# A two-layer encoder trunk in split fp32: Strassen's seven products for 18 of 22 up-projection pairs of the FFN

## Chip, cores and metric

One core of a Trainium2 chip runs the whole program. The metric is the device time of one execution in microseconds, as the median of several runs. Times of single instructions and waits come from one profiled execution of the kernel.

## The reference, cut to what matters

The trunk has two layers (DEPTH = 2). It is applied to 512 prompt tokens and 256 sample tokens, each with 1024 features. A layer is a mixer with four attention branches and gates, and then a gated FFN with a depthwise convolution of width 3 over the tokens. The change touches the FFN:

```python
def _conv_ffn(h, w_up, conv_w, conv_b, w_down):
    u = jnp.einsum('bsd,df->bsf', h, w_up)              # 1024 -> 2 * 2816
    up = jnp.pad(u, ((0, 0), (p, p), (0, 0)))           # p = 1
    c = conv_b
    for j in range(CONV_W):                             # CONV_W = 3
        c = c + up[:, j:j + S] * conv_w[j]
    gate, val = jnp.split(c, 2, axis=-1)
    return jnp.einsum('bsf,fd->bsd', jax.nn.gelu(gate, approximate=True) * val, w_down)
```

Around it stand an RMSNorm before (its output is h) and an RMSNorm and the residual add after. All of it is in float32.

## The kernel before

**Layout.** Features lie on the 128 partitions, and the 768 tokens of both groups side by side on the free axis. Each float32 operand x of a matrix product is split exactly into h = float32r(x) and l = x - h. ScalarE makes h by a copy (`copy`, L412) and VectorE makes l by a subtraction (`tt`, L426). A product is accumulated as h*h + h*l + l*h, which is three passes per block of 128 contraction rows. `mblock` issues, for each contraction block and pass, one matmul of 512 columns (prompt) and one of 256 (sample), all by `mm` (L396).

**Weights.** They come in units of [128, 1024] (`unit_keys`) through SyncE's one DMA queue (`dma`, L445) into two `raw` buffers (the two `bi` buffers serve as well at times). `pump` issues the load as soon as a buffer is free, and then splits the unit into one of four `w` buffers. An up-projection unit holds one block of 128 output features over all 8 contraction blocks.

**The FFN** (`ffn`, `up_pair`, `up_start`) has 22 hidden blocks f. For each there is a gate block (up unit f) and a value block (up unit f + 22), together a pair: 2 x 8 x 3 x 2 = 96 matmuls. `conv_block` brings an up block from PSUM through the convolution: a ScalarE copy with scale and bias (tap 1) and two VectorE operations (`stt`, L430; taps 0 and 2) for each token group. `glu` makes gelu(gate) * value and splits it into a `g` buffer. The hidden blocks are used in three parts (`THIRDS`: 7, 7 and 8 blocks). After a part's pairs come its eight output blocks of the down projection, which are added up in four `g` buffers:

```python
THIRDS = ((0, 7), (7, 14), (14, 22))
        for t, (a, b) in enumerate(THIRDS):
            ...
            for f in range(a0, min(b + 1, NF)):
                yield from self.up_pair(f, gs)
```

The last part goes through `grouped_tail`: its first two output blocks run over all tokens, the other six token group by token group, with the norm of each group started as it ends. Six weight units of that tail are split into parts of the next layer's `h` (`tail_h`, `Part`).

**What sets the order.** The program is emitted by generators (`Flow`), in the order of an estimate of the engines' times that is written in the kernel. The order within each engine's queue is then fixed: an engine works strictly along its list, and semaphores do the rest. Buffers have fixed numbers: 13 `g`, 12 `p` (of 512 columns), 4 `w`, 2 `raw`, 2 `bi`, one `h`; in PSUM two double banks `d` and four single banks `b`.

Of the kernel before, what the change touches and what calls it, by code (L numbers as in the profile page):

```python
# [17 lines left out]
F32 = mybir.dt.float32  # L18
# [44 lines left out]
def unit_keys():  # L63
    """The weight units of a layer in the order of their use."""
# [18 lines left out]
    for t, (a, b) in enumerate(THIRDS):  # L83
        a += t > 0
        for f in range(a, min(b + 1, NF)):
            u += [("up", f), ("up", f + NF)]
        u += [("down", t, m) for m in range(KB)]
    return u


def unit_data(key, w_in, w_branch, w_out, w_up, w_down):
    """The unit as [128, n]: contraction rows on partitions, then k block, then output column."""
# [28 lines left out]
    a, b = THIRDS[key[1]]  # L121
    return block(w_down[128 * a : 128 * b], 128 * key[2], 128 * key[2] + 128)


def unit_cols(key):
    if key[0] == "down":
        a, b = THIRDS[key[1]]
        return 128 * (b - a)
    return 1024


def host_arrays(inputs, depth):
# [31 lines left out]
    # rpb laid out by (column, row offset, key column), NEG outside the column window  # L164
# [8 lines left out]
    # constants of the shapes  # L173
# [30 lines left out]
# blocks of w_out and of the last third of the FFN that are computed token group by token group  # L204
# [42 lines left out]
class Slots:  # L247
    """The buffers of one tag: counts the live ones and knows when a free one may be written."""
# [51 lines left out]

class Pair:
    """Weights whose two parts lie in two buffers."""
# [13 lines left out]
class Part:  # L316
    """Weights in the columns of h whose tokens come to be known only after the weights' use."""
# [45 lines left out]
def mixed(a, b):  # L363
    """The elements of a and b, each in its order, evenly mixed, a first."""
# [4 lines left out]
class Trunk:  # L369
# [23 lines left out]
    def mm(self, out, lhsT, rhs, start, stop, *deps):  # L393
        n = out.shape[-1]
        ns = n * 0.4218 * (4 if lhsT.dtype == F32 else 1)
        self.nc.tensor.matmul(out=out, lhsT=lhsT, rhs=rhs, start=start, stop=stop)  # L396
# [55 lines left out]
    def w_init(self):  # L452
# [6 lines left out]
        self.tail_keys |= {("down", 2, m) for m in range(KB - TAIL_DOWN, KB)}  # L459
        self.w_total = self.depth * len(self.keys)  # L460

    def pump(self):
        while self.w_fetched < self.w_total and (self.RAW.freed or self.parts and self.BI.freed):
            n = self.w_fetched
            key = self.keys[n % len(self.keys)]
            tail = key in self.tail_keys
# [5 lines left out]
        while self.w_split < min(self.w_fetched, self.w_allowed):  # L472
            n = self.w_split
            raw, c, tail = self.w_raw[n]
            x = slice(0, c)
            src = raw[:, x]
            if raw.t > self.f.now + 300:
                break
            if tail and self.parts:
                w = self.parts.pop(0)  # L480
                src = src.rearrange("p (k x) -> p k x", x=GRP)
            elif self.W.freed:
                w = self.W.take([128, 2, 1024], F32R)
            elif self.spare and len(self.BI.freed) == 2:
                w = Pair([self.BI.take([128, 1024], F32R) for _ in range(2)])
            else:
                break
            del self.w_raw[n]
            t = self.copy(w[:, 0, x], src, raw.t, w.t)
            t = self.tt(w[:, 1, x], src, w[:, 0, x].bitcast(F32), ALU.subtract, t)  # L490
            w.t = t
            raw.drop(t)
            self.w_ready[n] = w
            self.w_split += 1

    def weight(self, key):
        n = self.w_used
        assert self.keys[n % len(self.keys)] == key, (key, self.keys[n % len(self.keys)])
        self.w_used += 1
        while n not in self.w_ready:  # L500
            self.pump()
            if n not in self.w_ready:
                raw = self.w_raw.get(n)
                yield max(self.f.now + 100, raw[0].t - 300 if raw else 0)
        w = self.w_ready.pop(n)
# [21 lines left out]

    def dblock(self):
# [3 lines left out]
    def bank(self):  # L532
        """A bank, of a double one or, if that leaves one for the norms, a single one."""
# [4 lines left out]
    def anyblock(self):  # L538
        """As dblock, but in two single banks if they are free sooner."""
# [1074 lines left out]
```

## Time and profile before

| | us |
|---|---|
| median of 3 runs (lowest to highest) | 2583.24 (2583.02 to 2583.34) |
| profiled execution, first to last instruction | 2580.6 |
| around that span (median less span) | 2.6 |
| TensorE matmuls busy | 2543.3 (99%) |
| VectorE busy | 1458.1 (57%) |
| ScalarE busy | 1133.5 (44%) |

The profile calls TensorE's matmuls PE and its weight loads PEld; DVE is VectorE, ACT is ScalarE and SP is SyncE, whose queue issues all DMAs. A busy share is the union of an engine's instructions over the span. Matmuls overlap each other, so the mean duration of one is longer than the time from one to the next. A name such as w<-raw tells which tile an instruction writes and reads, with buffer numbers left out. L396 is line 396 of the kernel.

The FFN of layer 0 runs from about 742 to 1240 us and that of layer 1 from about 2018 to 2514 us.

### The profile page before, as it was taken

Reading aid. Unit: us, or ns where it says so; the run is one execution under the profiler, and the core shown is the slowest. Engines: PE = TensorE matmul, PEld = TensorE weight load, DVE = VectorE, ACT = ScalarE, POOL = GpSimd, SP = SyncE. Lnnn points to the kernel's source line nnn. Section 1 sums busy time; section 2 is a strip of 40 time slices with the busy share of each in tenths; the row PEclk is TensorE's granted clock in tenths of the full one; section 3 lists DMA queues with packets and bytes.
Section 4 is the critical chain, followed back from the end, with each engine's and each line's share of the span. In section 5 each row is a group of like instructions: output and inputs, shape, how many; then the busy total and the mean of one; then the engine's idle time right before and its main releaser. Section 6 shows DMA issues by size and latency. Waiting matters only on the chain.

```text
span 2580.6 us, 39698 instructions
## 1 busy us (share of the span) xinstructions
PE 2543.3 (99%) x15964; PEld 2281.7 (88%) x15964; DVE 1458.1 (57%) x2766; ACT 1133.5 (44%) x2166; POOL 39.8 (2%) x38
## 2 busy tenths in 40 slices
PE   7999999999999999999999999999999999999998
PEld 7898888888998888888998988888889988888888
DVE  5567667746475335345566665775565752453554
ACT  5465666522463323233545556654225532331342
POOL 0001000000000000000000000000000000000000
PEclk9999999999999999999999999999999999999999
DMA  3333244433331111111333333443423212112122
GB/s 130 108 116 104 90 145 132 134 134 102 111 103 62 61 66 59 65 66 58 123 96 99 107 109 112 134 135 121 159 70 129 91 54 70 65 52 72 58 82 82
DMA packets 113576, 249.43 MB, mean 97 GB/s; under 512 B 13168, under 2 KB 56816, under 8 KB 113392
## 3 DMA queue, kind: packets, MB, share of 16 engines
q1 hardware_dynamic: 113392, 246.90, 29.7%
q8 instruction: 125, 2.05, 0.3%
q14 instruction: 59, 0.48, 0.1%
HBM read 194.15 MB, written 33.82 MB: 88 GB/s over the span
## 4 chain that ended last, share of the span: by engine, by line
PE 95%; DVE 3%; ACT 1%; issue 1%; DMA 0%; SPq 0%; POOLq 0%; DVEq 0%; ACTq 0%
PE d L396 78%; PE b L396 14%; PE b L400 3%; DVE g L426 1%; DVE p L426 1%; ACT p L412 1%; ACT g L412 0%; DVE h L426 0%; DVE w L426 0%; DVE p L967 0%; ACT w L412 0%; DMA par<-par 0%; ACT h L412 0%; DVE p L430 0%; SPq L445 0%
## 5 line engine op out<-in xcount | busy, mean ns | idle before, releaser
L396 PE MATMUL d<-h,w 128*128 128x512 f32 (+1 forms) x7248 | 1328.2, 338 | 0.0
L396 PEld LDWEIGHTS d<-h,w 128*128 128x128 f32 x7248 | 1106.4, 189 | 148.5
L426 DVE TENSOR_TENSOR w<-raw,w 128x1024 fp32r<-128x1024 f32 (+1 forms) x216 | 260.5, 1208 | 282.2 <-ACT w L412 271.2
L396 PE MATMUL d<-g,w 128*128 128x256 f32 (+1 forms) x2196 | 376.4, 329 | 1.6 <-ACT g L412 1.5
L430 DVE SCALAR_TENSOR_TENSOR p<-d,par,p 128x511 f32<-128x511 f32 (+1 forms) x328 | 204.3, 623 | 292.1 <-ACT p L412 286.3
L396 PEld LDWEIGHTS d<-g,w 128*128 128x128 f32 x2196 | 324.0, 189 | 43.3 <-ACT g L412 2.1
L412 ACT ACTIVATE p<-d,par 128x512 f32<-128x512 f32 (+1 forms) x164 | 111.1, 677 | 384.9 <-PE d L396 255.3
L412 ACT ACTIVATE w<-raw 128x1024 fp32r<-128x1024 f32 (+1 forms) x216 | 224.0, 1039 | 116.7 <-PE d L396 105.6
L412 ACT ACTIVATE p<-p,st 128x512 f32<-128x512 f32 (+2 forms) x288 | 178.1, 629 | 121.1 <-DVE st L994 67.9
L412 ACT ACTIVATE g<-d 128x128 fp32r<-128x128 f32 (+3 forms) x136 | 77.8, 574 | 284.7 <-PE d L396 247.9
L396 PE MATMUL d<-h,bi 128*128 128x256 f32 (+1 forms) x912 | 160.0, 334 | 0.0
L396 PEld LDWEIGHTS d<-h,bi 128*128 128x128 f32 x912 | 137.1, 189 | 19.1
L426 DVE TENSOR_TENSOR p<-b,p 128x512 fp32r<-128x512 f32 (+1 forms) x160 | 103.2, 658 | 63.1 <-ACT p L412 62.5
L412 ACT ACTIVATE p<-b 128x512 fp32r<-128x512 f32 (+1 forms) x160 | 90.6, 574 | 96.4 <-PE b L400 95.5
L396 PE MATMUL b<-g,g 128*128 128x512 f32 (+2 forms) x384 | 107.6, 356 | 2.7 <-DVE p L426 1.8
L396 PE MATMUL d<-g,bi 128*128 128x512 f32 (+1 forms) x636 | 107.7, 326 | 0.0
L396 PEld LDWEIGHTS d<-g,bi 128*128 128x128 f32 x636 | 93.0, 189 | 11.1
L396 PE MATMUL d<-w,h 128*128 128x256 f32 x672 | 93.7, 296 | 8.2 <-ACT h L412 3.4
L396 PE MATMUL b<-p,g 128*128 128x256 f32 x608 | 99.1, 287 | 1.1 <-DVE p L426 1.1
L412 ACT ACTIVATE g<-p 128x512 fp32r<-128x512 f32 x112 | 56.5, 540 | 98.1 <-DVE p L426 64.5
L967 DVE CUSTOM_DVE_ANT_0 p<-b,bi 128x512 f32<-128x512 f32 (+1 forms) x144 | 85.9, 597 | 22.5 <-PE b L396 18.1
L396 PEld LDWEIGHTS d<-w,h 128*128 128x128 f32 x672 | 88.3, 202 | 10.7 <-ACT h L412 4.0
(104 smaller groups left out, 2454.1 us busy)
## 6 DMA issues: line engine op xcount, KB each, us to landing
raw<-weights SPq DMA_DIRECT2D x236, 512.0 KB, 3.6
raw<-weights SPq DMA_DIRECT2D x32, 448.0 KB, 3.3
g<-g SPq DMA_DIRECT2D x128, 96.0 KB, 2.2
x<-g SPq DMA_DIRECT2D x36, 256.0 KB, 2.1
p<-x SPq DMA_DIRECT2D x36, 256.0 KB, 4.1
bi<-na_bias SPq DMA_DIRECT2D x64, 128.0 KB, 2.8
p<-x_in SPq DMA_DIRECT2D x24, 256.0 KB, 5.3
g<-g SPq DMA_DIRECT2D x16, 384.0 KB, 3.6
```

Source lines behind the costliest of these rows:

```text
L396: self.nc.tensor.matmul(out=out, lhsT=lhsT, rhs=rhs, start=start, stop=stop)
L400: self.nc.tensor.transpose(out=out, in_=in_, identity=self.ident)
L412: self.nc.scalar.activation(out=out, in_=in_, func=func, **k)
L426: self.nc.vector.tensor_tensor(out=out, in0=a, in1=b, op=op)
L430: self.nc.vector.scalar_tensor_tensor(out=out, in0=a, scalar=s, in1=b, op0=op0, op1=op1)
L967: nc.vector.tensor_tensor_reduce(out=p[:, :nkey], in0=s[:, :nkey], in1=bt, scale=1.0, scalar=init, op0=ALU.add, op1=ALU.max, accum_out=mx[ ...
```

## The change

Pairs 0 to 3 (`PLAIN = 4`) stay as they were. Pairs 4 to 21 are computed by `up_forms` with seven products in place of eight (Strassen's scheme in Winograd's form). The contraction is halved (512 and 512 rows), the tokens are halved (`TH` = 384 columns), and gate block and value block are the two halves of the output. A product is 4 contraction blocks x 3 passes = 12 matmuls of 384 columns (`mprod`), and a pair is 84 matmuls.

- `forms` makes, once per layer, four differences of h's quarters (8 `g` buffers, kept till the last pair).
- `preparer` makes, for each pair, four sums and differences of the weights' quarters on VectorE, and splits seven weight blocks in place of eight.
- `up_forms` brings the products together in an SBUF buffer u: four ScalarE copies out of PSUM and three VectorE adds of PSUM onto u, each of 384 columns. Two PSUM regions, x and z, each accumulate several products in turn, with a copy or an add between them.
- Each gate block goes through convolution and gelu (`gate_block`). For ten hidden blocks (`WHOLE`) the value block is convolved and multiplied at once, and the product goes to DRAM. For the other twelve the gelu and the raw value block go to DRAM, and the value's convolution is done on return (`value_block`, `g_load`).
- All 22 pairs now come before the down projection. It has five parts (`CHUNKS`: 2, 8, 2, 2 and 8 blocks). `g_loader` fetches the hidden blocks from DRAM in that order, each into a `g` buffer when one is free. The eight blocks of the second part (`BANK`) go into the `h` buffer, once the up projection has ended. The last part goes through `grouped_tail` as before.
- `calm` holds back an instruction for VectorE while the estimate has more than 0.5 us queued there.

```diff
-THIRDS = ((0, 7), (7, 14), (14, 22))
+WHOLE = (0, 1, 6, 8, 10, 12, 14, 16, 18, 20)
+CHUNKS = (WHOLE[:2], WHOLE[2:], (2, 3), (4, 5), (7, 9, 11, 13, 15, 17, 19, 21))
+BANK = WHOLE[2:]
+PLAIN = 4
+TH = T // 2
...
+    def preparer(self):
...
+            done(w, (yield from self.calm_split(w, all_, raw.ap, raw.t)))
...
+            t = self.tt(s1.ap, raw2[:, lo], raw2[:, hi], ALU.add, raw2.t, s1.t)
+            t2 = self.tt(s2.ap, s1.ap, raw[:, lo], ALU.subtract, t, s2.t)
+            yield from self.calm_split(w, hi, s2.ap, t2)
+            done(w, (yield from self.calm_split(w, lo, s1.ap, t)))
+            yield from self.calm()
+            t = self.tt(raw2[:, lo], raw[:, lo], raw2[:, lo], ALU.subtract)
+            t2 = self.tt(s1.ap, raw[:, hi], s2.ap, ALU.subtract)
...
+            t = yield from self.calm_split(w, all_, raw2.ap, t)
...
+            t = yield from self.calm_split(w, lo, s1.ap, t2)
...
+    def mprod(self, out, w, i, rhs, start):
+        for k in range(4):
+            c = 512 * i + 128 * k
+            for n, (a, b) in enumerate(self.PASSES):
+                t = self.mm(out, w[:, a, c : c + 128], rhs(k, b), start and k == 0 and n == 0,
+                            k == 3 and n == 2, more=not start)
...
+    def up_forms(self, f):
...
+        x, z, y1 = d[:, 0:TH], d[:, 512 : 512 + TH], y[:, 0:TH]
+        t = yield from self.mprod(x, w, 0, quarter(0, lo), True)
+        t1 = self.copy(u[:, 0, lo], x, t, u.t)
+        t = yield from self.mprod(y1, w, 1, quarter(4, lo), True)
...
+        t1 = self.tt(u[:, 0, lo], u[:, 0, lo], y1, ALU.add, t, t1)
...
+        t = yield from self.mprod(x, w, 1, summed(1), False)
+        t2 = self.copy(u[:, 0, hi], x, t, u.t)
...
+        t = yield from self.mprod(z, w, 0, summed(0), True)
...
+        t3 = self.copy(u[:, 1, hi], z, t, u.t)
...
+        t = yield from self.mprod(x, w, 0, summed(2), False)
+        t3 = self.tt(u[:, 1, hi], u[:, 1, hi], x, ALU.add, t, t3)
...
+        t = yield from self.mprod(z, w2, 0, quarter(4, hi), False)
...
+        t2 = self.tt(u[:, 0, hi], u[:, 0, hi], z, ALU.add, t, t2)
+        self.up_done(f, Summed(u, 0, max(t1, t2)))
...
+        t = yield from self.mprod(x, w, 1, summed(3), False)
...
+        t4 = self.copy(u[:, 1, lo], x, t, u.t)
...
+    def g_load(self, f, q, c0, c1, box):
...
+        v.t = t = self.dma(v[:, 0:n], dv[:, c0:c1], v.t)
+        if f not in WHOLE:
+            a.t = self.dma(a[:, 0:n], da[:, c0:c1], a.t)
...
+            t = yield from self.conv(f + NF, v[:, 0:n], c, n, v.t)
...
+            t = self.tt(c[:, 0:n], c[:, 0:n], a[:, 0:n], ALU.mult, t, a.t)
...
+        t = self.copy(q.ap[:, 0, c0:c1], c[:, 0:n], t, q.t)
...
+        t = self.tt(q.ap[:, 1, c0:c1], c[:, 0:n], q.f32()[:, 0, c0:c1], ALU.subtract, t)
...
     def ffn(self, gain, sandwich, box):
         gs = [[] for _ in range(NF)]
...
+        yield from self.up_start()
+        for f in range(2, PLAIN):
+            yield from self.up_pair(f)
+        self.f.start(self.g_loader(gs), 2)
+        for f in range(PLAIN, NF):
+            yield from self.up_forms(f)
...
+        for n, fs in enumerate(CHUNKS):
```

**TensorE in one pair of layer 0.** In the up projection before, the matmuls alternate between 512 and 256 columns through a block, and 48 of them make a block (d152 is the gate block of pair 11, w107 its weights):

```order
L396 MATMUL d152_11058<-h2_6736,w103_10807 128x512
L396 MATMUL d152_11058<-h2_6736,w103_10807 128x256
L396 MATMUL d153_11129<-h2_6736,w104_10877 128x512 [waits DVE_49,Activation_49]
L396 MATMUL d153_11129<-h2_6736,w104_10877 128x256
L396 MATMUL d153_11129<-h2_6736,w104_10877 128x512
```

Now pair 17 reads as follows (d119 holds x and z, b313 is y1, g91 to g98 are the differences of h, w106 to w108 and g127 the prepared weights):

```order
L441 MATMUL d119_10091<-h2_6736,w106_9979 128x384 x12
L441 MATMUL b313_10092<-h2_6736,w106_9979 128x384 x12
L441 MATMUL d119_10091<-g93_8123,w107_9995 128x384 [waits Activation_49]
L441 MATMUL d119_10091<-g93_8123,w107_9995 128x384 x5
L441 MATMUL d119_10091<-g94_8148,w107_9995 128x384 x6
L441 MATMUL d119_10091<-g91_7860,w107_9995 128x384 [waits Activation_49]
L441 MATMUL d119_10091<-g91_7860,w107_9995 128x384 x5
L441 MATMUL d119_10091<-g92_7885,w107_9995 128x384 x6
L441 MATMUL d119_10091<-g95_8185,w108_10041 128x384 [waits Activation_49]
L441 MATMUL d119_10091<-g95_8185,w108_10041 128x384 x5
L441 MATMUL d119_10091<-g96_8207,w108_10041 128x384 x6
L441 MATMUL d119_10091<-h2_6736,g127_10062 128x384 [waits DVE_49]
```

A product's twelve matmuls now stand together, and where x or z is used again the first matmul waits for ScalarE's copy or VectorE's add of the product before.

**VectorE ahead of the last part of the down projection, layer 0.** Before, these are the rows from the convolution of the last value block (d157, pair 21) to the split of its product into g115, the last hidden block of the last part:

```order
L430 SCALAR_TENSOR_TENSOR p471_11465<-d157_11396,par0_103,p471_11465 128x511 [waits Activation_49]
L430 SCALAR_TENSOR_TENSOR p471_11465<-d157_11396,par0_103,p471_11465 128x511 [waits DVE_49]
L430 SCALAR_TENSOR_TENSOR p472_11469<-d157_11396,par0_103,p472_11469 128x255 [waits Activation_49]
L430 SCALAR_TENSOR_TENSOR p472_11469<-d157_11396,par0_103,p472_11469 128x255 [waits DVE_49]
L426 TENSOR_TENSOR h3_11458<-raw131_11350,h3_11458 128x4x256 [waits DMAHW7_49,Activation_49]
L426 TENSOR_TENSOR h3_11458<-raw132_11420,h3_11458 128x4x256 [waits DMAHW0_49,Activation_49]
L426 TENSOR_TENSOR p471_11465<-p466_11399,p471_11465 128x512
L426 TENSOR_TENSOR p472_11469<-p467_11403,p472_11469 128x256 [waits DVE_49,Activation_49]
L426 TENSOR_TENSOR g115_11511<-p471_11465,g115_11511 128x512 [waits Activation_49]
L426 TENSOR_TENSOR g115_11511<-p472_11469,g115_11511 128x256 [waits Activation_49]
```

Now the last two additions of the fourth part (d154, d155) are followed by the splits of six weight units (h4, w151 and w152; the first two rows of h4 stand ahead and between) and then by the second half of block 17 (g150):

```order
L471 TENSOR_TENSOR g141_10965<-g141_10965,d154_11955 128x768 [waits PE_49]
L471 TENSOR_TENSOR h4_11658<-raw122_11933,h4_11658 128x4x256 [waits DMAHW0_49,Activation_49]
L471 TENSOR_TENSOR g141_10965<-g141_10965,d155_11978 128x768 [waits PE_49]
L471 TENSOR_TENSOR h4_11658<-raw123_11952,h4_11658 128x4x256 [waits DMAHW1_49,Activation_49]
L471 TENSOR_TENSOR h4_11658<-bi63_11973,h4_11658 128x4x256 [waits DMAHW2_49,Activation_49]
L471 TENSOR_TENSOR w151_12025<-bi64_11975,w151_12025 128x1024 [waits DMAHW3_49,Activation_49]
L471 TENSOR_TENSOR w152_12040<-raw124_11993,w152_12040 128x1024 [waits DMAHW4_49,Activation_49]
L475 SCALAR_TENSOR_TENSOR p564_11821<-p563_11820,par0_103,p564_11821 128x255
L475 SCALAR_TENSOR_TENSOR p564_11821<-p563_11820,par0_103,p564_11821 128x255 [waits DVE_49]
L471 TENSOR_TENSOR p564_11821<-p564_11821,p565_11822 128x256 [waits DVE_49]
```

After eight rows for block 19 (g151) and one weight unit (bi66), block 21 (g152) follows, fetched from DRAM (p575 and p578 hold its value block, p577 and p580 its gelu):

```order
L471 TENSOR_TENSOR bi66_12069<-raw125_12015,bi65_12068 128x1024 [waits DMAHW5_49,Activation_49]
L471 TENSOR_TENSOR g151_11814<-p570_11831,g151_11814 128x256 [waits Activation_49]
L471 TENSOR_TENSOR g151_11814<-p567_11826,g151_11814 128x512
L475 SCALAR_TENSOR_TENSOR p576_12052<-p575_12051,par0_103,p576_12052 128x511 [waits DMAHW6_49,Activation_49]
L475 SCALAR_TENSOR_TENSOR p576_12052<-p575_12051,par0_103,p576_12052 128x511 [waits DVE_49]
L471 TENSOR_TENSOR p576_12052<-p576_12052,p577_12053 128x512 [waits DMAHW7_49,DVE_49]
L475 SCALAR_TENSOR_TENSOR p579_12073<-p578_12072,par0_103,p579_12073 128x255 [waits DMAHW1_49,Activation_49]
L475 SCALAR_TENSOR_TENSOR p579_12073<-p578_12072,par0_103,p579_12073 128x255 [waits DVE_49]
L471 TENSOR_TENSOR p579_12073<-p579_12073,p580_12074 128x256 [waits DMAHW2_49,DVE_49]
L471 TENSOR_TENSOR g152_11999<-p576_12052,g152_11999 128x512 [waits Activation_49]
L471 TENSOR_TENSOR g152_11999<-p579_12073,g152_11999 128x256 [waits Activation_49]
```

Block 21 stands behind all of these in VectorE's list, and the fetch for it starts when the fourth part has given back a `g` buffer. Before, nothing but the convolution of the last pair and two splits stood there.

**TensorE at the same place.** The first output block of the last part (d156) uses blocks 7, 9, 11, 13, 15, 17, 19 and 21 in turn, six matmuls each:

```order
L441 MATMUL d156_12000<-g151_11814,w149_11943 128x512 [waits DVE_49]
L441 MATMUL d156_12000<-g151_11814,w149_11943 128x256
L441 MATMUL d156_12000<-g151_11814,w149_11943 128x512
L441 MATMUL d156_12000<-g151_11814,w149_11943 128x256
L441 MATMUL d156_12000<-g152_11999,w149_11943 128x512 [waits Activation_49]
L441 MATMUL d156_12000<-g152_11999,w149_11943 128x256 [waits Activation_49]
L441 MATMUL d156_12000<-g152_11999,w149_11943 128x512 [waits DVE_49]
```

Three hidden blocks are waited for one after the other, where the rows of before have no wait but the one for g115.

## Rows read from the trace of the kernel before

**Rows 1.** The page: span, TensorE's busy time, and the chain that ended last.

```profile
span 2580.6 us, 39698 instructions
...
PE 2543.3 (99%) x15964; PEld 2281.7 (88%) x15964; DVE 1458.1 (57%) x2766; ACT 1133.5 (44%) x2166; POOL 39.8 (2%) x38
...
PE 95%; DVE 3%; ACT 1%; issue 1%; DMA 0%; SPq 0%; POOLq 0%; DVEq 0%; ACTq 0%
```

**Rows 2.** Windows inside both FFNs: length, busy us (instructions) by engine, clock, DMA.

```profile
core 0: us, PE busy (x) PEld busy (x) DVE busy (x) ACT busy (x) POOL busy (x), PEclk, DMA share, GB/s
800.00:1200.00 400.00, 400.00 (x2266) 346.96 (x2265) 180.28 (x258) 126.12 (x191) 0.00 (x0) 1.00 0.18 62
2100.00:2400.00 300.00, 300.00 (x1700) 260.07 (x1699) 123.94 (x173) 88.45 (x131) 0.00 (x0) 1.00 0.18 62
```

**Rows 3.** TensorE's waits, 742 to 1240 (2018 to 2513 alike): total, times, longest.

```profile
PE d L396 <- ACT g L412: 0.7, 1, 0.7
```

**Rows 4.** Groups by form, TensorE: shape, count, busy us, mean ns, idle before.

```profile
L396 PE MATMUL d<-h,w 128*128 128x512 f32 x3480 | 1249.0, 399 | 0.0
L396 PE MATMUL d<-h,w 128*128 128x256 f32 x3768 | 1012.3, 281 | 0.0
...
L396 PE MATMUL b<-g,g 128*128 128x384 f32 x64 | 16.5, 340 | 0.0
```

**Rows 5.** Groups by form, VectorE.

```profile
L426 DVE TENSOR_TENSOR w<-raw,w 128x1024 fp32r<-128x1024 f32 x190 | 232.2, 1224 | 263.2 <-ACT w L412 252.2 <-PE b L400 9.2
L430 DVE SCALAR_TENSOR_TENSOR p<-d,par,p 128x511 f32<-128x511 f32 x172 | 129.0, 750 | 239.9 <-ACT p L412 236.9
...
L430 DVE SCALAR_TENSOR_TENSOR p<-d,par,p 128x255 f32<-128x255 f32 x156 | 75.4, 483 | 52.2 <-ACT p L412 49.4
...
L426 DVE TENSOR_TENSOR g<-p,g 128x512 fp32r<-128x512 f32 x68 | 46.9, 689 | 19.7 <-ACT g L412 19.7
...
L426 DVE TENSOR_TENSOR h<-g,h 128x512 fp32r<-128x512 f32 x36 | 22.4, 682 | 0.0
...
L426 DVE TENSOR_TENSOR g<-g,d 128x768 f32<-128x768 f32 x16 | 15.3, 954 | 72.8 <-PE d L396 72.8
```

**Rows 6.** Groups by form, ScalarE.

```profile
L412 ACT ACTIVATE w<-raw 128x1024 fp32r<-128x1024 f32 x190 | 199.5, 1052 | 90.0 <-PE d L396 79.0 <-PE b L396 10.6
...
L412 ACT ACTIVATE p<-d,par 128x512 f32<-128x512 f32 x86 | 67.0, 779 | 259.8 <-PE d L396 255.3 <-DVE p L430 4.5
...
L412 ACT ACTIVATE g<-d 128x768 f32<-128x768 f32 x40 | 32.5, 812 | 200.5 <-PE d L396 200.4
```

**Rows 7.** Timeline, end of layer 0's up projection: start, length, [idle before, releaser].

```profile
1219.54 7.58 PE L396 MATMUL d<-g,w 128*128 128x512 f32 x42
1219.74 0.78 ACT L412 ACTIVATE p<-d,par 128x512 f32<-128x512 f32 x1 [4.58 <-PE d L396]
1220.56 1.53 DVE L430 SCALAR_TENSOR_TENSOR p<-d,par,p 128x511 f32<-128x511 f32 x2 [4.14 <-ACT p L412]
...
1224.19 2.36 DVE L426 TENSOR_TENSOR h<-raw,h 128x1024 fp32r<-128x1024 f32 x2 [0.47 <-ACT h L412]
...
1226.47 1.02 DVE L426 TENSOR_TENSOR p<-p,p 128x512 f32<-128x512 f32 x2
1227.19 0.94 ACT L412 ACTIVATE g<-p 128x512 fp32r<-128x512 f32 x2 [1.78 <-DVE p L426]
...
1227.87 1.45 PE L396 MATMUL d<-g,w 128*128 128x512 f32 x4 [0.74 <-ACT g L412]
```

**Rows 8.** Windows at the turn from layer 0 to layer 1.

```profile
1300.00:1318.70 18.70, 17.71 (x149) 17.45 (x148) 14.94 (x33) 10.38 (x28) 1.36 (x2) 1.00 0.24 82
1318.70:1322.10 3.40, 3.35 (x17) 3.05 (x17) 1.38 (x5) 3.01 (x9) 0.70 (x1) 0.50 0.00 0
1322.10:1325.50 3.40, 1.63 (x11) 1.23 (x11) 3.40 (x7) 2.77 (x7) 0.00 (x0) 1.00 0.00 0
1325.50:1328.90 3.40, 3.40 (x19) 3.40 (x18) 1.39 (x4) 0.28 (x1) 0.00 (x0) 0.51 0.02 5
```

**Rows 9.** The page: DMA issues, KB each, us from issue to landing.

```profile
raw<-weights SPq DMA_DIRECT2D x236, 512.0 KB, 3.6
...
p<-x SPq DMA_DIRECT2D x36, 256.0 KB, 4.1
```

More of the change, by code (lines that the diff above doesn't have):

```diff
@@ L82, in unit_keys, with unit_steps @@
     u += [("out", m) for m in range(KB)]
[L83 to L86, printed above, removed]
+    for f in range(NF):
+        u += [("up", f), ("up", f + NF)]
+    for t in range(len(CHUNKS)):
         u += [("down", t, m) for m in range(KB)]
     return u
+def unit_steps(keys, depth):
+    steps = []
+    for l in range(depth):
+        for n, key in enumerate(keys):
+            n += l * len(keys)
+            if key[0] != "up" or key[1] % NF < PLAIN:
+                steps.append(("unit", n))
+            elif key[1] < NF:
+                steps += [(s, n) for s in ("first", "sums", "last", "rest")]
+    return steps
 def unit_data(key, w_in, w_branch, w_out, w_up, w_down):
@@ L458, in w_init @@
         self.tail_keys = {("out", m) for m in range(KB - TAIL_OUT, KB)}
-        self.tail_keys |= {("down", 2, m) for m in range(KB - TAIL_DOWN, KB)}
+        self.tail_keys |= {("down", len(CHUNKS) - 1, m) for m in range(KB - TAIL_DOWN, KB)}
         self.w_total = self.depth * len(self.keys)
+        self.steps = unit_steps(self.keys, self.depth)
+        self.paired = {n + i for s, n in self.steps if s == "first" for i in range(2)}
     def pump(self):
-        while self.w_fetched < self.w_total and (self.RAW.freed or self.parts and self.BI.freed):
+        while self.w_fetched < self.w_total:
             n = self.w_fetched
             key = self.keys[n % len(self.keys)]
+            more = self.parts or self.spare and n in self.paired
+            if not (self.RAW.freed or more and self.BI.freed):
+                break
             tail = key in self.tail_keys
@@ L471, in pump @@
             self.w_fetched += 1
[L472 to L493, printed above, removed]
-            self.w_split += 1
+        while self.w_split < min(len(self.steps), self.w_allowed) and self.step(*self.steps[self.w_split]):
+            self.w_split += 1
@@ new lines, in split, with step @@
+    def split(self, w, x, src, *deps):
+        t = self.copy(w[:, 0, x], src, *deps, w.t)
+        return self.tt(w[:, 1, x], src, w[:, 0, x].bitcast(F32), ALU.subtract, t)
+    def step(self, kind, n):
+        if kind != "unit" or n not in self.w_raw or self.w_raw[n][0].t > self.f.now + 300:
+            return False
+        raw, c, tail = self.w_raw[n]
+        x = slice(0, c)
+        src = raw[:, x]
+        if tail and self.parts:
+            w = self.parts.pop(0)
+            src = src.rearrange("p (k x) -> p k x", x=GRP)
+        elif self.W.freed:
+            w = self.W.take([128, 2, 1024], F32R)
+        elif self.spare and len(self.BI.freed) == 2:
+            w = Pair([self.BI.take([128, 1024], F32R) for _ in range(2)])
+        else:
+            return False
+        del self.w_raw[n]
+        w.t = t = self.split(w, x, src, raw.t)
+        raw.drop(t)
+        self.w_ready[self.w_split] = w
+        return True
@@ new lines, in g_load @@
+    def g_load(self, f, q, c0, c1, box):
+        while f not in self.a_dram or f not in self.v_dram:
+            yield self.f.now + 300
+        (da, ta), (dv, tv) = self.a_dram[f], self.v_dram[f]
+        yield max(ta, tv)
+        n = c1 - c0
+        yield from self.P.wait(1 if f in WHOLE else 3)
+        c = v = self.P.take([128, TP], F32)
+        if f not in WHOLE:
+            c, a = (self.P.take([128, TP], F32) for _ in range(2))
+        v.t = t = self.dma(v[:, 0:n], dv[:, c0:c1], v.t)
+        if f not in WHOLE:
+            a.t = self.dma(a[:, 0:n], da[:, c0:c1], a.t)
+        yield t
+        if f not in WHOLE:
+            t = yield from self.conv(f + NF, v[:, 0:n], c, n, v.t)
+            v.drop(t)
+            yield a.t
+            yield from self.calm()
+            t = self.tt(c[:, 0:n], c[:, 0:n], a[:, 0:n], ALU.mult, t, a.t)
+            a.drop(t)
+            yield t - self.f.HOP
+        t = self.copy(q.ap[:, 0, c0:c1], c[:, 0:n], t, q.t)
+        yield t - self.f.HOP
+        yield from self.calm()
+        t = self.tt(q.ap[:, 1, c0:c1], c[:, 0:n], q.f32()[:, 0, c0:c1], ALU.subtract, t)
+        c.drop(t)
+        box.append((q, t))
@@ new lines, in g_loader @@
+    def g_loader(self, gs):
+        order = sum(CHUNKS, ())
+        for n, f in enumerate(order):
+            if f in BANK:
+                if f == BANK[0]:
+                    while not self.up_over:
+                        yield self.f.now + 300
+                    self.H_old.drop()
+                    bank = self.H_old = self.H.take([128, len(BANK), 2, T], F32R)
+                q = Slice(bank, BANK.index(f))
+            else:
+                q = yield from self.G.get([128, 2, T], F32R)
+            while sum(len(gs[i]) < 2 for i in order[:n]) > 2:
+                yield self.f.now + 200
+            for c0, c1 in ((0, TP), (TP, T)):
+                self.f.start(self.g_load(f, q, c0, c1, gs[f]), 0 if self.up_over else 2)
@@ L1385, in ffn @@
                     blk.drop(tt)
-                for f in range(a, b):
-                    gs[f][0].drop()
+                if fs == BANK:
+                    self.tail_h()
             else:
@@ L1566, in main @@
         self.w_init()
+        self.f.start(self.preparer(), 3)
         self.new_h()
```

299 lines of the change are left out of this document (220 added, 79 removed).

## The prediction, on record before the changed kernel ran

> **What bounds the kernel now.** I read the page first. TensorE's matmuls are busy for 99% of the span, and the chain that ended last runs 95% through TensorE [rows 1]. Then I looked at the FFN, where the change lies. In 400 us of layer 0's FFN and 300 us of layer 1's TensorE is never idle, at full clock, while VectorE is busy 45% and 41% of the time [rows 2]. In the whole FFN of a layer TensorE waits once, for 0.7 us [rows 3]. So each matmul that goes saves its full time, as long as the other engines keep up, and the questions are what the new work puts on VectorE and where TensorE will have to wait for it.
>
> One matmul costs 400 us / 2266 = 176.5 ns from one to the next, and half of these are 512 columns wide and half 256 [rows 2]: 384 on average. The mean durations are 399 and 281 ns, and the few matmuls of 384 columns last 340 ns, which is just the middle [rows 4]. So I take 176.5 ns for one of 384 columns as well.
>
> **What the change removes.** A pair goes from 96 matmuls to 84. Over 18 pairs and two layers that is 36 x 12 = 432 matmuls fewer, and 432 x 0.1765 = **76.2 us**. The down projection keeps its matmuls (22 blocks x 8 outputs x 3 passes x 2 widths). A pair takes 84 x 0.1765 = 14.83 us, where it took 16.94.
>
> **What it adds on VectorE in the up projection.** Two neighbouring pairs, one of them WHOLE, take 29.65 us on TensorE. VectorE's list between two equal places holds 38 instructions for them: 4 of 1024 columns, 15 of 512, 6 of 384, one of 256, and 6 each of 511 and 255 with a parameter. With 1.224, 0.689, 0.750 and 0.483 us from [rows 5], and 0.556 and 0.42 for 384 and 256 on the line through 512 and 768, that is 4.90 + 10.34 + 3.34 + 0.42 + 4.50 + 2.90 = 26.4 us, 89% of the time. Instructions that follow each other directly take less: 36 of 682 ns have a union of 22.4 us, not 24.6 [rows 5], which is 0.08 us for each of the 27 that follow one. With that the 26.4 become some 24.5. So VectorE keeps up, but it goes from 45% to over 80%. ScalarE has far less to do (its dearest operations are 0.78 to 1.05 us [rows 6]).
>
> Work that TensorE waits for directly is short. x and z are used again one product later, that is 12 x 0.1765 = 2.1 us later, and in between stands one copy (some 0.5 us, for 384 of the 768 columns that take 0.812 [rows 6]) or one add (0.56). The weights of a pair are prepared during the pair before, some 10 us ahead. So I take **no wait in the steady stretch**. The bounds are 0 below and some 0.5 us a pair (18 us) above, if one handover of each pair is late by that.
>
> **What it adds at the first Strassen pair.** VectorE has to make four differences and their splits (16 operations of 768 columns, 0.95 us each, 15 us) besides the convolution of pairs 0 to 3. Its list from the end of the norm to the first new add is 61 instructions, 47 us by the same rows, against 49.4 us on TensorE: the last token group of pairs 0 and 1 (96 matmuls of 256 columns, at two thirds of 176.5 ns 11.3 us), pairs 2 and 3 (33.9) and two products (4.2). It just fits. I take 1 us a layer (0 to 4), because the first pair needs a PSUM double bank that pair 3 gives back late.
>
> **What it adds in the down projection.** The second part needs eight blocks from DRAM in the h buffer, which is free only when the up projection ends. But the first part (two blocks, 8 x 2.12 = 16.9 us) runs first. A fetch lands 4.1 us after its issue [rows 9], and the eight splits (1.1 us each on VectorE) and the first weight unit fit in that. I take 1.3 us a layer (0 to 5), for the weight unit, whose load stands on SyncE's queue behind two stores that wait for pair 21's gelu.
>
> **The last part** is where I expect the cost. Before, the last value block is the only thing late: its copy starts 0.2 us after the last part has begun on TensorE at 1219.54, the chain goes over VectorE (with two weight splits of 2.36 us together in it), and TensorE, which reaches that block after 7 x 1.06 = 7.4 us, goes on at 1227.87 after a wait of 0.74 [rows 7]. A handover between engines costs little there: the copy ends at 1220.52, and VectorE begins at 1220.56. Now three blocks (17, 19 and 21) stand behind the fourth part's last additions in VectorE's list. Let 0 be the end of the fourth part on TensorE.
> - A split that stands ahead of the last addition ends at 1.0, and the addition (0.95 [rows 5]) at 1.9.
> - Then come four weight splits. The load of the last of them is issued when a buffer comes back at 1.0, lands at 4.6 [rows 9], is copied by ScalarE till 5.7 (1.05 [rows 6]) and split till 6.9.
> - Then 21 instructions: 6 of 255 and 4 of 511 columns, 6 of 256, 4 of 512, one of 1024. By durations 2.90 + 3.00 + 2.52 + 2.76 + 1.22 = 12.4 us, and about 1.0 less for those that overlap: 11.4. So block 21 is ready at 18.3.
> - TensorE's last six matmuls end at 19.0 instead of 8.5: a wait of **10.5 us**, in three pieces of 3 to 5 us.
>
> Less the 0.7 of before, that is 9.8 us. In layer 1 no weights of a next layer stand there (one split of 1.1 less): 8.7. Together 18.5 us. As bounds I take 0, if the weights come early and the splits run while TensorE still works on the fourth part, and 15 us a layer, if the fetch of block 21 is issued late too.
>
> Waits of that kind also cost clock. At the turn of the layers the clock fell to 0.50 for 3.4 us after TensorE had been busy for only 17.71 of 18.70 us, and again after 1.63 of 3.40 [rows 8]. A spell of 3.4 us at 1.2 GHz instead of 2.4 costs 1.7 us. With one or two spells I take 2.5 us a layer, 5 in all (0 to 7).
>
> **The sum.** 2580.6 - 76.2 + 18.5 + 5.0 + 2 x (1.0 + 1.3) = 2532.5 us for the span, and 2.6 us lie around it (the median of the runs less the span): **2535 us**, 1.9% faster. Loads and stores through DRAM cost nothing in this sum: the queue moves 62 GB/s at a share of 0.18 in the FFN [rows 2]. A pair adds at most 1.6 MB, written and read, to its 1 MB of weights, and a fetch stands tens of us behind its store. If that cover is gone, a weight load comes late behind a store that waits. The preparation has some 10 us to spare there.
>
> **The rivals.**
> - *The late blocks are hidden.* For it speaks that the emitting order was made with all these pieces in view. Against it, VectorE's list is fixed and the four splits stand behind the last addition. Then only the 76 us remain, less what the two starts cost: 2507 to 2520 us. Chance 0.20.
> - *VectorE sets the pace of the up projection.* Its 26.4 us need only 3.3 us of idle time in two pairs to pass TensorE's 29.65, and in such a stretch of its list it has six waits for a product and some eighteen for a copy. With 0.2 us each (4.8 us) the two pairs take 31.2 us, 1.55 more, and 18 of those are 28 us: 2563; the case spans 2552 to 2582. Against it, idle time before splits is time in which nothing was due [rows 5], and handovers are short [rows 7]. Chance 0.17. A rule speaks for this rival: the Trainium skill (VectorE: DVE Perf Modes, section Terms) has a pipeline flush after every VectorE operation, before whose end the next can't issue. By it the 26.4 us would stand in full, and the last part would wait 1 us longer in each layer (2537 in the sum above). The trace disagrees, with 22.4 us for 36 operations of 682 ns [rows 5].
> - *A matmul of 384 columns costs more than the middle*, say 190 ns, which the 64 short-lived ones of the trace can't exclude. The saving falls to 36 x (16.94 - 15.96) = 35 us: 2576. Chance 0.04.
> - *Slower than before: the reuse of x and z.* In a pair x is overwritten after a copy twice and after an add once, and z after a copy once, and each copy or add stands in the fixed list of an engine behind weight work of up to 1.22 us apiece. If two such operations stand ahead of it, the next product waits. It decides when these waits pass (76.2 - 28.1) / 36 = 1.34 us a pair. Three late handovers of 0.6 us would make 1.8 us a pair, 65 us: 2600. For it speaks that VectorE is at over 80%. Against it, in the rows of the list one to four small instructions stand between a product and its add, and there are 2.1 us for them. Chance 0.06.
>
> **How the numbers follow.** The forecast keeps 0.53, and its own range is 2520 to 2552 (the bounds of the small terms and half of those of the last part). The range of 2507 to 2567 takes in the hidden case and the nearer half of VectorE's. What a measurement of this kernel can tell from no change is about 0.2%, or 5 us. All cases but the last end well below that: faster 0.93, slower 0.06, and 0.01 between.
>
> **What would show it.** In the profile after, TensorE should have 432 matmuls fewer (15,532), with 340 ns for 384 columns, and pairs 14.8 us apart with no waits inside. VectorE's busy share in a stretch of the up projection should be 80 to 89%. TensorE should wait some 10 us for blocks 17, 19 and 21 at the last part of each layer, released by VectorE and ScalarE on g, with the clock at 0.5 nearby. I am wrong if waits stand inside the pairs (the second or the fourth rival), if a pair takes more than 15 us without waits (the third), or if the last part waits less than 3 us (the first).

## The result, and the profile after

The changed kernel takes 2681.46 us (median of four runs, 2680.35 to 2690.11), against 2583.26 for the kernel before: a ratio of 1.0389, interval 1.0374 to 1.0404. It is 3.9% slower, where the prediction had 1.9% faster, and the range did not hold it. The profiled execution is the longest of the four (span 2688.3), so the differences below sum to 107.8 us, where the medians differ by 98.2.

First the page of the kernel after: span, busy time, and the chain that ended last [rows 1].

```profile
span 2688.3 us, 40398 instructions
...
PE 2516.4 (94%) x15532; PEld 2283.9 (85%) x15532; DVE 1723.7 (64%) x3222; ACT 1279.3 (48%) x2474; POOL 39.8 (1%) x38
...
PE 84%; DVE 8%; ACT 4%; issue 2%; DMA 1%; SPq 0%; DVEq 0%; POOLq 0%; ACTq 0%
```

TensorE has 432 matmuls fewer, as expected. But its share of the chain fell from 95% to 84%, and VectorE and ScalarE took the place. Neither is overloaded, at 64% and 48%.

Next, where the time went. I cut the profiled executions by number of matmuls: after the 4,668 ahead of a layer's FFN, after as many as the up projection has (2,112 before, 1,896 with seven products), and after the down projection's 1,056. The time is from the start of the first matmul of a stage to that of the next stage. Before, the first two parts of the down projection stand between the pairs, so there the two FFN rows divide the same number of matmuls and not the two projections themselves. The matmuls of both have the same two widths, 512 and 256.

| stage, us | before | after | difference | predicted |
|---|---|---|---|---|
| layer 0, ahead of the FFN | 733.4 | 734.7 | +1.3 | 0 |
| layer 0, up projection | 363.7 | 395.2 | +31.5 | -37.1 |
| layer 0, down projection | 169.8 | 184.8 | +15.0 | +13.6 |
| turn of the layers | 17.4 | 17.4 | 0 | 0 |
| layer 1, ahead of the FFN | 725.0 | 739.4 | +14.4 | 0 |
| layer 1, up projection | 363.7 | 398.3 | +34.6 | -37.1 |
| layer 1, down projection | 169.8 | 180.8 | +11.0 | +12.5 |

In layer 1's up projection the clock stood at 0.50 for 6.8 us from 2142.8 on, and that stage is 3.1 us longer than layer 0's. The down projection came out within 1.5 us a layer of its terms. The up projection missed by about 70 us a layer, and layer 1's attention, which the change doesn't touch, by 14. Now the up projection's stretch in the windows of the kernel after [rows 2]:

```profile
820.00:1120.00 300.00, 251.58 (x1349) 231.15 (x1348) 196.06 (x302) 131.30 (x225) 0.00 (x0) 1.00 0.25 82
```

The clock is full and VectorE is busy 65% of the time, less than the 80 to 89% of the prediction. TensorE is idle for 48 of 300 us. Here is what it waited for in the Strassen pairs of layer 0 (803 to 1130 us; total, times, longest) [rows 3]:

```profile
PE d L441 <- ACT g L457: 29.9, 36, 1.6
PE d L441 <- DVE g L471: 23.8, 35, 0.7
```

That is 71 waits in 18 pairs, where four in each would be 72: two for ScalarE's copy out of PSUM into u (a `g` buffer) and two for VectorE's add. The timeline of one pair shows them (start, length, what was done, and the idle time before with its releaser):

```profile
951.07 2.24 PE L441 MATMUL d<-g,w 128*128 128x384 f32 x12
...
953.77 0.63 ACT L457 ACTIVATE w<-p 128x512 fp32r<-128x512 f32 x1 [2.14 <-DVE p L471]
954.31 0.47 ACT L457 ACTIVATE g<-d 128x384 f32<-128x384 f32 x1
...
954.84 2.37 PE L441 MATMUL d<-g,w 128*128 128x384 f32 x12 [1.52 <-ACT g L457]
...
957.24 0.49 ACT L457 ACTIVATE g<-d 128x384 f32<-128x384 f32 x1 [1.63 <-PE d L441]
...
957.78 2.35 PE L441 MATMUL d<-g,w 128*128 128x384 f32 x12 [0.58 <-ACT g L457]
```

At 951.07 a product goes to x, at 954.84 the next one to z, at 957.78 the next to x. The product for z starts 0.06 us after the copy of x has ended (954.31 + 0.47), and the next one for x starts right after the copy of z. Here no product covers a copy. That is also to be read in the order ahead of the prediction: the first product into z (the row with d119 and g91) is marked as waiting for ScalarE, although nothing in z has to be saved at that point. I had read these marks as the waits for x or z itself. x and z are two halves of one tile d of 1,024 columns, and the waits were set for the tile, not for its halves.

Last, layer 0's down projection: its waits for hidden blocks (1138 to 1323 us), nearly all in its last part, and the window of its half clock [rows 8]:

```profile
PE d L441 <- ACT g L457: 7.3, 4, 5.3
PE d L441 <- DVE g L471: 1.9, 3, 1.3
```

```profile
1262.20:1279.20 17.00, 11.46 (x29) 7.83 (x30) 12.53 (x24) 7.43 (x15) 0.00 (x0) 0.50 0.24 77
```

These waits are 9.2 us in all, and the clock was at 0.50 for 17 us, from within the longest of them (1258.8 to 1264.05) on.

### The profile page after: what moved, and what is told of

It reads as the page before. It is cut to its first block, busy times and chain, and to the rows that moved or that the text cites. A ratio compares the mean times of both kernels' runs of the same rounds, so it can differ in the third digit from the quotient of the medians.

```text
span 2688.3 us, 40398 instructions
## 1 busy us (share of the span) xinstructions
PE 2516.4 (94%) x15532; PEld 2283.9 (85%) x15532; DVE 1723.7 (64%) x3222; ACT 1279.3 (48%) x2474; POOL 39.8 (1%) x38
## 4 chain that ended last, share of the span: by engine, by line
PE 84%; DVE 8%; ACT 4%; issue 2%; DMA 1%; SPq 0%; DVEq 0%; POOLq 0%; ACTq 0%
PE d L441 66%; PE b L441 15%; DVE g L471 4%; PE b L445 3%; ACT g L457 2%; DVE p L471 2%; ACT w L457 2%; DVE w L471 1%; ACT p L457 1%; DVE p L475 1%; DMA p<-v 1%; DVE h L471 0%; DMA bi<-weights 0%; DVE p L1087 0%; DMA raw<-weights 0%
## 5 line engine op out<-in xcount | busy, mean ns | idle before, releaser
L441 PE MATMUL d<-h,w 128*128 128x512 f32 (+2 forms) x5616 | 1042.6, 337 | 0.6 <-DVE w L471 0.6
L441 PEld LDWEIGHTS d<-h,w 128*128 128x128 f32 x5616 | 867.0, 189 | 101.3 <-DVE w L471 1.2
L441 PE MATMUL d<-g,w 128*128 128x384 f32 (+2 forms) x3504 | 641.7, 335 | 101.1 <-ACT g L457 75.1
L441 PEld LDWEIGHTS d<-g,w 128*128 128x128 f32 x3504 | 558.6, 191 | 168.4 <-ACT g L457 103.1
L457 ACT ACTIVATE g<-d 128x384 f32<-128x384 f32 (+4 forms) x278 | 147.2, 530 | 354.8 <-PE d L441 318.3
L471 DVE TENSOR_TENSOR g<-g,d 128x384 f32<-128x384 f32 (+2 forms) x159 | 101.2, 641 | 194.8 <-PE d L441 194.7
L441 PE MATMUL b<-h,w 128*128 128x384 f32 (+2 forms) x960 | 167.6, 329 | 0.0
L441 PEld LDWEIGHTS b<-h,w 128*128 128x128 f32 x960 | 151.6, 189 | 8.5
L475 DVE SCALAR_TENSOR_TENSOR p<-g,par,p 128x511 f32<-128x511 f32 (+1 forms) x208 | 128.2, 616 | 47.0 <-ACT p L457 41.9
L441 PE MATMUL d<-h,g 128*128 128x384 f32 x432 | 85.2, 345 | 25.7 <-DVE g L471 25.7
```

Of the source, the lines that this page charges most:

```text
L457: self.nc.scalar.activation(out=out, in_=in_, func=func, **k)
L471: self.nc.vector.tensor_tensor(out=out, in0=a, in1=b, op=op)
L475: self.nc.vector.scalar_tensor_tensor(out=out, in0=a, scalar=s, in1=b, op0=op0, op1=op1)
```

## The experiments

Theory A: x and z count as one tile, so every handover between TensorE and the engine that empties PSUM lies open. Theory B: ScalarE and VectorE are late because their lists are full.

**z in a tile of its own.**

```diff
+        zb = yield from self.B.get([128, 512], F32)
-        x, z, y1 = d[:, 0:TH], d[:, 512 : 512 + TH], y[:, 0:TH]
+        x, z, y1 = d[:, 0:TH], zb[:, 0:TH], y[:, 0:TH]
...
         t2 = self.tt(u[:, 0, hi], u[:, 0, hi], z, ALU.add, t, t2)
+        zb.drop(t2)
```

> The four products of a pair that go to x and z now write two separate PSUM tiles (z in a single bank b of its own) instead of the two banks of one tile d. The order on every engine stays as it is. Theory A (in the kernel as changed, x and z count as one tile, so each product waits for the copy or add of the product just before it, although that one reads the other bank): the gaps of 0.6 to 1.5 us ahead of four products of each pair go, pairs come 14.8 to 15.4 us apart instead of 18.75, that is 36 x 3.4 to 3.9 = 122 to 141 us less: 2540 to 2560 us. Theory B (ScalarE and VectorE are themselves late, because their lists are full of weight work): the gaps stay or move, pairs stay above 18 us apart, and the time falls by less than 25 us, to 2655 or more. Between the two: VectorE becomes the bound once TensorE no longer waits, with pairs at 15.5 to 16.5 us and 2565 to 2600 us.

Measured: 2532.84 us, a ratio to before of 0.981 (0.9791 to 0.9829): 148.6 us less than the changed kernel, from an edit of three lines that moves no instruction on any engine. Its windows, and a piece of its timeline at the same place of the pair as above:

```profile
820.00:1060.00 240.00, 240.00 (x1386) 239.75 (x1386) 197.33 (x307) 132.37 (x229) 0.00 (x0) 1.00 0.35 111
2080.00:2300.00 220.00, 220.00 (x1271) 220.00 (x1270) 184.48 (x285) 123.14 (x212) 0.00 (x0) 1.00 0.35 109
```

```profile
945.50 2.24 PE L441 MATMUL d<-g,w 128*128 128x384 f32 x12
...
947.58 2.24 PE L441 MATMUL b<-g,w 128*128 128x384 f32 x12
...
948.74 0.47 ACT L457 ACTIVATE g<-d 128x384 f32<-128x384 f32 x1
...
949.66 2.24 PE L441 MATMUL d<-g,w 128*128 128x384 f32 x12
949.94 0.48 ACT L457 ACTIVATE g<-b 128x384 f32<-128x384 f32 x1
```

Products start 2.08 us apart and TensorE is never idle. The copy of x at 948.74 now runs beside the product into z (now a tile b). In the order, the first product into z is without a wait:

```
L441 MATMUL d119_10104<-g94_8148,w107_10008 128x384 x6
L441 MATMUL b327_10106<-g91_7860,w107_10008 128x384 x6
L441 MATMUL b327_10106<-g92_7885,w107_10008 128x384 x6
L441 MATMUL d119_10104<-g95_8185,w108_10054 128x384 [waits Activation_49]
```

Theory A holds, and VectorE, now at 82%, is not the bound. The time is 7 us below the expected range, as a pair takes 84 x 240.00 / 1386 = 14.55 us.

**Less on VectorE, one tile as before.** The weight sums are left out, so gate and value are computed from raw weight quarters, and the layer's results are no longer those of the FFN.

```diff
-            t = self.tt(s1.ap, raw2[:, lo], raw2[:, hi], ALU.add, raw2.t, s1.t)
-            t2 = self.tt(s2.ap, s1.ap, raw[:, lo], ALU.subtract, t, s2.t)
-            yield from self.calm_split(w, hi, s2.ap, t2)
-            done(w, (yield from self.calm_split(w, lo, s1.ap, t)))
+            yield from self.calm_split(w, hi, raw[:, hi], t2)
+            done(w, (yield from self.calm_split(w, lo, raw[:, lo], t)))
...
-            t = self.tt(raw2[:, lo], raw[:, lo], raw2[:, lo], ALU.subtract)
-            t2 = self.tt(s1.ap, raw[:, hi], s2.ap, ALU.subtract)
```

> x and z stay in one tile. The four sums and differences of weight quarters of each pair are left out (raw quarters are split in their place), which takes 4 operations of 512 columns, 4 x 0.69 = 2.8 us a pair, from VectorE. Theory A (one tile): the handovers are as before, pairs stay 18 to 19 us apart, and the time stays within 15 us of 2681. Theory B (VectorE is late): pairs come 1.5 to 2.8 us closer, that is 54 to 100 us less, 2580 to 2630.

Measured: 2658.59 us (one run), 23 less. That is outside A's 15 us and far from B's 54 to 100. The up projection takes 384.8 us a layer against 320.4 with z apart, so an open handover still costs (384.8 - 320.4) / 72 = 0.89 us with the sums gone, where it cost (395.2 - 320.4) / 72 = 1.04. Nearly all of it is the chain itself. About 0.15 us is queueing behind weight work, as in the timeline above, where the copy of x stood behind a split. The timeline of all 18 pairs of layer 0 says the same: in the changed kernel this copy starts 0.55 us after its product has ended on average, and without the sums 0.04. At the other three handovers the copy or add starts 0.04 to 0.11 us after its product in both kernels, and the next product still starts 0.85 to 0.99 us late.

**Two open handovers in place of four.**

```diff
-        x, z, y1 = d[:, 0:TH], d[:, 512 : 512 + TH], y[:, 0:TH]
+        x, z, y1 = d[:, 0:TH], zb[:, 0:TH], d[:, 512 : 512 + TH]
```

> x and y1 share the two banks of one tile d, and z has a tile of its own. Then two handovers of a pair lie open instead of four or none: the second product (y1) waits for the copy of x, and the third (x) for the add of y1; z and the later uses of x have a product between them. With pairs 18.75 us apart at four open handovers and 14.62 at none, one costs (18.75 - 14.62) / 4 = 1.03 us. Theory A (each open handover costs that, wherever it stands): pairs 16.7 us apart and 2533 + 36 x 2.06 = 2607 us (2595 to 2620). Theory B (something particular to z in the second bank of d made the difference, not the count of open handovers): within 10 us of 2533, or of 2681.

Measured: 2599.23 us (one run), with these waits between 750 and 1130 us:

```profile
PE d L441 <- DVE g L471: 12.2, 18, 0.7
PE d L441 <- ACT g L457: 11.1, 18, 0.7
PE d L441 <- DVE w L471: 0.3, 1, 0.3
```

Two a pair, as expected, since 36 waits in 18 pairs of layer 0 stand in place of 71 (the third row is one wait for weights). The up projection takes 353.7 us a layer: (353.7 - 320.4) / 36 = 0.93 us for each open handover, a little less than in the changed kernel. Zero, two and four of them give 320, 354 and 395 us. So it is their number that counts, and nothing particular to z.

**The way through DRAM alone.** No pair uses the seven products, and the differences of h are not made. The fetches from DRAM still start at pair 4.

```diff
-PLAIN = 4
+PLAIN = NF
```

> No pair uses the seven products (all 22 are computed with 96 matmuls); what remains of the change is the way of all hidden blocks through DRAM, the five parts of the down projection and the later convolution of twelve value blocks. If the balance of the changed kernel is read rightly (2583 - 76 for the matmuls + 141 for the gaps in the pairs + about 33 for the rest = 2681), this one takes 2583 + 33 = 2616 us (2605 to 2630), with some 9 us of waits and 13 to 17 us at half clock at the last part of each layer. If the way through DRAM costs nothing by itself: 2580 to 2590.

Measured: 2619.06 us (one run), 37 more than before, of which 14.5 and 11.2 in the down projections and 11.4 in layer 1's attention. The 2,112 matmuls of the up projection take 363.7 us a layer, what the first 2,112 of the FFN took before: loads and stores through DRAM cost them nothing.

**Blocks 17, 19 and 21 multiplied before they go to DRAM.**

```diff
-WHOLE = (0, 1, 6, 8, 10, 12, 14, 16, 18, 20)
+WHOLE = (0, 1, 6, 8, 10, 12, 14, 16, 18, 20, 17, 19, 21)
-CHUNKS = (WHOLE[:2], WHOLE[2:], (2, 3), (4, 5), (7, 9, 11, 13, 15, 17, 19, 21))
+CHUNKS = (WHOLE[:2], WHOLE[2:10], (2, 3), (4, 5), (7, 9, 11, 13, 15, 17, 19, 21))
```

> Blocks 17, 19 and 21, the last three of the last part, are convolved and multiplied before they go to DRAM, so on their return VectorE has two splits a block instead of seven operations (15 of the 21 instructions go from that place, about 7 us). Theory A (VectorE's list is what the last part waits for): the waits there fall from 9 us to 4 or less and the clock stays at half for less than 10 us a layer; 15 to 25 us less than 2681. Theory B (the fetch of these blocks is issued or lands late, whatever VectorE has to do): the waits stay at 7 us or more and the time within 8 us of 2681.

Measured: 2658.05 us (one run), 23 less than the changed kernel. The waits of layer 0's down projection (1138 to 1308 us) are down to this row:

```profile
PE d L441 <- DVE g L471: 1.4, 1, 1.4
```

The clock no longer falls there, and the down projections take 170.1 and 170.3 us, against 169.8 before. So VectorE's list was what the last part waited for, and the half clock came with those waits. The edit also takes away the fetches of three gelus, but late fetches are not the cause. In the changed kernel the last fetch for block 21 is issued at 1263.12 us and has landed by 1266.4, and VectorE comes to that block at 1269.66:

```profile
1259.82 1.23 DVE L471 TENSOR_TENSOR w<-bi,w 128x1024 fp32r<-128x1024 f32 x1 [2.29 <-ACT w L457]
...
1263.12 0.37 SPq L490 DMA_DIRECT2D p<-a  x1
...
1269.66 1.53 DVE L475 SCALAR_TENSOR_TENSOR p<-p,par,p 128x511 f32<-128x511 f32 x2
```

The first of these rows is the one longer stop of VectorE there: 2.29 us ahead of a weight split, for ScalarE's copy of that unit.

**Layer 1's attention.** Compared by shape, place by place, the order of TensorE's matmuls ahead of the FFN is in the kernel before the same in both layers but for 60 of the 4,668, all among the first 216. With the change 1,080 differ. The kernel without the seven products (the way through DRAM alone) has the changed kernel's order in layer 1's attention, and its loss there of 11.4 us, so the products have no part in it. In the trace of the kernel with z apart, a projection's weights sit in the two bi buffers until 1335.4 us, and only then are the loads of the attention's bias issued (a view of the tile bi: count, shortest, median and longest in ns, first and last start):

```profile
L441 PEld LDWEIGHTS d<-h,bi x48: 187/188/190, 1327.1 to 1335.4; 128*128 128x128 f32 x48
...
L490 SPq DMA_DIRECT2D bi<-alibi x2: 328/376/424, 1335.6 to 1335.9; - x2
```

That is 71.3 us after the layer's start, where it was 58.7 before (1351.74 - 1293.0). The rule that forbids it for the units of q, k and the gates (z keeps its own tile):

```diff
-        elif self.spare and len(self.BI.freed) == 2:
+        elif self.spare and len(self.BI.freed) == 2 and self.keys[n % len(self.keys)][0] not in "kqg":
             w = Pair([self.BI.take([128, 1024], F32R) for _ in range(2)])
```

> z has its own tile, and one more rule: a weight unit of the attention's projections is not put into the two bi buffers. In the kernel as changed one such unit of layer 1 sits there until 1335.6 us, and the load of the attention's bias into them waits for it; from there the order of layer 1's attention differs from that of layer 0, and layer 1's attention takes 737.7 us where the kernel before has 725.0. With the rule the order of layer 1's attention is that of layer 0 again. Theory A (that order costs the 12 us): layer 1's attention takes 724 to 727 us and the whole 2533 - 12 = 2521 (2517 to 2525). Theory B (the 12 us come from elsewhere, such as the turn of the layers or the clock): 2530 to 2536.

Measured: 2523.46 us, ratio 0.9769 (0.9756 to 0.9783). Layer 1's attention takes 726.6 us, the bias loads are issued 60.2 us after the layer's start, and the two layers' orders differ in 60 matmuls again. Theory A holds: the emitter put a unit where the attention needed room, and the order behind it cost 11 us. TensorE's idle time in that stage is 13.3 us with z apart, 8.0 with the rule and 5.5 before, and with the rule it has two spells of 3.4 us at half clock fewer. That the emitter did so because estimated times at the turn of the layers had shifted is argued and not shown.

**All three together.**

> All three together: z in its own tile, no attention weights in the bi buffers, and blocks 17, 19 and 21 convolved and multiplied before they go to DRAM. If the parts add up: 2533 - 12 - 23 = 2498 us (2490 to 2506), with the down projection at 170 us a layer as in the kernel before, and VectorE 85 to 90% busy in the last pairs of the up projection. If VectorE becomes the bound there, since it has 15 more operations to do for those three pairs than before: waits of TensorE for x, z or the weights near the end of the up projection and 2505 to 2520.

Measured: 2501.28 us (2496.70 to 2502.32), ratio 0.9686 (0.9673 to 0.9699), 3.1% faster than before. The down projections take 169.1 and 169.4 us. Its windows show VectorE at 84 and 85% with TensorE hardly idle:

```profile
820.00:1060.00 240.00, 239.43 (x1380) 238.25 (x1379) 201.44 (x317) 135.60 (x235) 0.00 (x0) 1.00 0.33 101
2080.00:2300.00 220.00, 219.43 (x1265) 217.77 (x1264) 186.56 (x296) 126.72 (x223) 0.00 (x0) 1.00 0.34 104
```

## Why the prediction was wrong

- **The step that failed** is "x and z are used again one product later, that is 2.1 us later", and with it "no wait in the steady stretch" (bounds 0 to 0.5 us a pair). It was right for the data and wrong for the tile: z's product also waited for x's copy, x's for z's. Four handovers a pair lay open at about 1.04 us each, 4.2 us a pair. With the 14.55 us of TensorE's work a pair took 18.75, and 36 x 4.2 = 151 us were lost in all. Giving z its own tile returned 148.6.
- A handover was priced at nearly nothing by the gap it leaves (0.04 us from one engine to the next [rows 7]). An open one is the whole chain: the copy or add of 0.47 to 0.55 us, and the end and the start of a run of matmuls. In the timeline above, products start 957.78 - 954.84 = 2.94 us apart in place of 2.08. Of those 0.86 us only 0.58 shows as idle time. Some 0.16 is the overlap of one product's last matmul with the next one's first (2.24 less 2.08), which is lost, and some 0.13 the longer product itself (2.37 against 2.24).
- **The rival on the other side** named the place (the reuse of x and z) and had 0.06. Its mechanism was another one, copies that stand in a queue. That is worth some 0.15 us a handover, and the rest of its price, which passed the 1.34 us a pair from which it decides, came from the tile.
- **The matmul term** was right in count and a little low: seven products save 363.7 - 320.4 = 43.3 us a layer, 86.6 in all, against 76.2. A matmul of 384 columns costs 240.00 / 1386 = 173.2 ns, not the 176.5 of the mean of 512 and 256.
- **The two starts** cost next to nothing, where 1.0 and 1.3 us a layer were reckoned: with z apart TensorE waits nowhere in layer 0's up projection (763 to 1062 us), and with blocks 17, 19 and 21 multiplied early the down projection takes 170.1 us against 169.8.
- **The last part** was right in place and cause: waits of 9.2 us in layer 0 against 10.5, behind VectorE's list, with blocks 17, 19 and 21 as the cause (the edit that took the work away took the wait). Its chain was 3 us too short: the four weight splits end 9.4 us after the fourth part and not 6.9 (the stop of 2.29 us is in there), and block 21 is ready after 21.4 us and not 18.3. That the wait is no longer for it agrees with TensorE's matmuls there taking longer at half clock. The clock term was low in time at half clock (17 us against one or two spells of 3.4), yet waits and clock together gave 15.0 and 11.0 us against 13.6 and 12.5. The way through DRAM cost nothing in the up projection, as predicted.
- **VectorE's pace** was the second likeliest rival (0.17), and it didn't happen even when TensorE ran without a stop. It is busy 197.33 of 240 us there, which is 23.9 us for two pairs of 29.1, near the 24.5 reckoned with overlap. The durations of its instructions in that window add up to 209.8 us, which is 25.4 for two pairs, so they do overlap. The rule of the Trainium skill (VectorE: DVE Perf Modes, section Terms), by which the 26.4 us would stand in full, is not what the trace shows.
- **Left out altogether**: layer 1's attention, +14 us. I had priced only the stages that the diff touches, but an order that is emitted from an estimate of times can change anywhere behind an edit. Comparing the orders of the two layers shows ahead of any run that it did, though not what that costs.
- The forecast of 2535 us lies close to the kernel with z apart (2532.84), but partly by luck: 10 us more saved in the pairs stand against 12.7 us lost in layer 1's attention.

For reading PSUM while a matmul runs, the Trainium skill (PSUM — Partial Sum Buffer, section Summary: rules for kernel authors) tells authors to target a different bank. The runs agree as far as they go: with z apart, ScalarE copies out of d while TensorE writes b (948.74 above) without a loss. What kept TensorE from writing one half of d while the other was read was the order's waits.

## What to carry to other kernels

Two regions that are to be filled and emptied in turn need tiles of their own, if waits are set by the tile: a double buffer inside one tile is none. Read each wait in the order as a question (which earlier instruction is it for, and does this one need it?), and price an open handover as the whole chain of stop, copy and start, some 0.9 us here, times its count. And when the order comes from an estimate, compare it in the stages that the edit doesn't touch as well.

## What was not expected of the hardware

Twelve matmuls of 384 columns take 2.08 us (945.50 to 947.58), where six of 512 and six of 256 take 12 x 0.1765 = 2.12: the even width is 2% cheaper for the same columns. And the busy time of TensorE hides part of a stall: the changed kernel's 15,532 matmuls are busy for 2516.4 us with the open handovers and, on this page of the kernel with z apart, for 46 us less:

```profile
PE 2470.7 (98%) x15532; PEld 2283.2 (90%) x15532; DVE 1721.5 (68%) x3222; ACT 1277.6 (50%) x2474; POOL 39.8 (2%) x38
```

With few overlaps between neighbours, the union of the same matmuls is longer, so idle time alone understates what a wait costs. 144 open handovers at 0.16 + 0.13 us make 42 of the 46 us (an estimate from the one handover above); a part of the difference is also clock, as the mean granted clock of the two executions is 0.987 and 0.991.
